# A fused encoder layer: smaller descriptor memory, own bytes for two attention tiles, token scales through DRAM, first tokens in pairs

## The chip, the cores and the metric

The kernel runs on one core of one Trainium2 chip. A core has five engines that run their own instruction streams: TensorE (PE, matrix products; its weight loads are listed as PEld), VectorE (DVE), ScalarE (ACT), GpSimd (POOL) and SyncE (SP), which here issues nearly all DMA transfers. The metric is the device time of one execution in microseconds (us); of several runs the median counts.

## The reference

The kernel computes one layer of a bidirectional encoder for 1280 tokens of width 1024: a prompt of 1024 tokens and a second sequence of 256 that shares the weights. Cut to what matters here:

```python
n = rms_norm(h, g_mix)
qa, ka, va, qb, kb, vb = split(n @ w_in)
# mixer A: 4 heads, two softmax maps each, combined with lambda
sc = einsum(qa, ka) * scale - slope * abs(qpos - kpos)
oa = rms_norm((softmax(sc[0]) - lam * softmax(sc[1])) @ va, g_subln)
# mixer B: 8 query heads on 2 key/value heads
qb, kb = rope(rms_norm(qb, g_qnorm)), rope(rms_norm(kb, g_knorm))
ob = softmax(einsum(qb, kb) * scale) @ vb
h = h + concat(oa, ob) @ w_out
h = h + relu(rms_norm(h, g_mlp) @ w_ff1) ** 2 @ w_ff2
h = h + gate(rms_norm(h, g_ple)) * (p @ w_ple_proj)
return rms_norm(h)
```

All in float32. The norm before the projection is a scale by `g_mix` for each column and by a scalar for each token, the token scale `rstd1`.

## The kernel before, in words

**Arithmetic.** Each float32 operand is split into a high and a low part (`xh`/`xl`, `whp`/`wlp`, `nhi`/`nlo`): ACT writes the high part, DVE (or POOL) the difference. A product is three matmuls, high by high, high by low and low by high (`split3`, L156; `mm_gen`, L225).

**Order.** The program is written with generators that are interleaved; a scheduler with its own timeline then fixes each engine's order, so a change in one place can move rows elsewhere. An engine runs its row in order: an instruction that waits holds everything behind it. SP's transfers use eight semaphores in turn, so each also waits for the one eight before it.

**Start.** `load_w` (L175, L176) loads weights (`rawp`) in pieces of two 128-row blocks and splits them; `load_x` (L239, L240) loads the transposed tokens (`xr`) and makes `xh` (with the scale `gmix`) and `xl`. The first 256 tokens are loaded as two pieces of two blocks and one of four. The unit for the keys and values of mixer B (`b_unit(2, ...)`, output `psb`) takes the first two token blocks together, in two pieces of 12 matmuls each and block. Beside it runs the unit for mixer A's values (`psv`).

**Token scales.** `R` is the row of 1280 token scales on all 128 partitions. It is made with ten diagonal matrices `dg` (DVE, L429), ten products with a matrix of ones (PE, `psr`, L430; 20 records, two for each) and three copies (ACT, L431). Its reader is the eviction `zl<-psa,R` of mixer A's projections (L369, L747).

**Attention.** Keys, queries and values go through DRAM (`kd`, `qd`, `vad`, `vbd`) and come back as tiles `kt`, `qt`, `vt`. Scores `sc` (L559) go to a softmax chain on DVE (`mm`, `rl`), ACT (`p`, `ph`) and POOL, then transposes `tr` (L613) and products with the values (`av`, L637). Keys of mixer B are `kd_72`, its first queries `qd_64` and `qd_65`; mixer A's first are `kd_68` and `qd_60`. `dist` is the table of distances.

**MLP.** The first MLP product is done on quarters of the operands with seven products (i = 1 to 7) for each of 16 pieces p of 256 columns. `mlp_sums` forms sums of transposed tokens (`nb`, `nt`), `n_split` splits them; POOL's DMAs copy parts into `nlo` (L1006). Weight pieces `w1r` (L979) are loaded in turn into the slots W8, W9, W10, multiplied with `gmlp` by POOL (L1046), combined (`w1s`) and split into `w` (L1054, L1055). Products `f_...` are gathered in the tiles `q`, in slots Q0 to Q3 (ACT L1170, DVE L1172 to L1186). Q0 to Q3 and W10 are in one pool `fq` that opens when the pool of `nt` and `nb` closes.

Of the kernel before, what the change touches and what calls it, by code (L numbers as in the profile page):

```python
# [45 lines left out]
def encoder_kernel(ctx: ExitStack, tc: tile.TileContext, x, xT, pT, w_in, w_out, w_ff1, w_ff2, w_gate, w_proj,  # L46
# [44 lines left out]
    def load(*args):  # L91

        with tc.issue_after(chain[-1].ins) if chain else contextlib.nullcontext():
            chain[:] = [dma(*args)]
        return chain[0]
# [32 lines left out]
        return t  # L128

    gmix = cp.tile([P, KD], F32, name="gmix")  # L130
    gmlp = cp.tile([P, KD], F32, name="gmlp")

    neglam = cp.tile([P, 1], F32, name="neglam")
# [19 lines left out]
    def split3(ps, pairs, start=True, stop=True):  # L153
        n = len(pairs)
        for i, (a, b) in enumerate(pairs):
            PE.matmul(ps, a, b, start=start and i == 0, stop=stop and i == n - 1)  # L156
# [5 lines left out]
    def load_w(src, cols, n, rawp, wp, tag, lo_eng, between={}, dma=dma):  # L162

        c0 = cols
        hi, lo = [], []
        kn = 512 // n
        kw = {"bufs": WHB} if n == 256 else {}
        for kk in range(KD // kn):
            if kk in between:
                between[kk]()  # L170
            raw = rawp.tile([P, kn, n], F32, tag="raw", name=f"raw{tag}", bufs=RAWB if n == 256 else 2)
            w_dma[:] = [dma(raw, src[kk * kn * P:(kk + 1) * kn * P, c0:c0 + n].rearrange("(k p) c -> p k c", p=P))]
            a = wp.tile([P, kn, n], F32R, tag="wh", name=f"wh{tag}", **kw)
            b = wp.tile([P, kn, n], F32R, tag="wl", name=f"wl{tag}", **kw)
            S.activation(a, raw, AF.Copy)  # L175
            lo_eng.tensor_tensor(b, raw, f(a[:]), op=ALU.subtract)  # L176
            hi += [a[:, i, :] for i in range(kn)]
            lo += [b[:, i, :] for i in range(kn)]
        return hi, lo


    xs = ExitStack()
# [13 lines left out]
    def pj(name):  # L196
        return ppj.tile([P, 512], F32, tag="pj", name=name)
# [34 lines left out]
    def load_x(t0, n, ks=KD, k1=0, kn=4, dma=dma, tag="xr"):  # L232
        for k0 in range(k1, k1 + ks, kn):
            xr = bp.tile([P, kn, n], F32, tag=tag, name="xr", bufs=2)
            dma(xr, xT[k0 * P:(k0 + kn) * P, t0:t0 + n].rearrange("(k p) t -> p k t", p=P))
            if t0 == k0 == 0:
                load(gmix, g_mix)
            for k in range(k0, k0 + kn):
                S.activation(xh[:, k, t0:t0 + n], xr[:, k - k0], AF.Copy, scale=gmix[:, k:k + 1])  # L239
                V.scalar_tensor_tensor(xl[:, k, t0:t0 + n], xr[:, k - k0], gmix[:, k:k + 1], f(xh[:, k, t0:t0 + n]),  # L240
                                       op0=ALU.mult, op1=ALU.subtract)
# [9 lines left out]
    def tok_pairs(w, t):  # L251
        wh, wl = w
        c = slice(t * P, (t + 1) * P)
        pr = []
        for k in range(KD):
            pr += [(xh[:, k, c], wh[k]), (xh[:, k, c], wl[k]), (xl[:, k, c], wh[k])]
        return pr
# [33 lines left out]
    def b_unit(u, w, hook=None):  # L291

        kv = u == 2
        npair = 1 if kv else 2
        pend = collections.deque()
        pss = {}

        def finish(c0, cn, trp):
            for m in range(npair):
                hl = (bp.tile([P, 2, 512], F32R, tag="qkl", name="qkl", bufs=1) if kv  # L300
                      else bp.tile([P, 2, 512], F32R, tag="xr", name="qkl", bufs=2))
                S.activation(hl[:, 0, :cn], trp[m][:, :cn], AF.Copy)
                V.tensor_tensor(hl[:, 1, :cn], trp[m][:, :cn], f(hl[:, 0, :cn]), op=ALU.subtract)
                dst = kd[4] if kv else qd[4 + 2 * u + m]
                dma(dst[:, :, c0:c0 + cn].rearrange("v p t -> p v t"), f(hl[:, :, :cn]))

        def tr(args):
            o, t, c0, cn, trp = args
            for m in range(npair):
                PE.transpose(trp[m][:, t * P - c0:t * P - c0 + P], o[:, m * P:(m + 1) * P], ident)  # L310
            if (t + 1) * P == c0 + cn:
                finish(c0, cn, trp)

        for (c0, cn) in TCH:
            trp = None
            for t in range(c0 // P, (c0 + cn) // P):
                if hook:
                    hook(t)
                tag = "tr1" if kv and t in (2, 3) else "pb"
                ps = pss.pop(t, None) or pp1.tile([P, 512], F32, tag=tag, name="psb", bufs=2)  # L320
                if kv and t == 0:

                    pss[1] = pp1.tile([P, 512], F32, tag="pb", name="psb", bufs=2)
                    for kh, u_ in itertools.product(range(2), range(2)):
                        split3((ps, pss[1])[u_][:, :256], tok_pairs(w, u_)[12 * kh:12 * kh + 12], kh == 0, kh == 1)
                        yield 1.0
                elif not kv or t != 1:
                    yield from mm_gen(ps[:, :256], tok_pairs(w, t))
                o = norm_rope(ps, t, 2 if kv else 4, gk if kv else gq)
                if kv:  # L330
                    hl = bp.tile([P, 2, 2, 64], F32R, tag="vbl", name="vbl")
                    vps = ps[:, 128:256].rearrange("p (h d) -> p h d", d=64)
                    r1 = rstd1[:, t:t + 1]
                    S.activation(hl[:, :, 0, :], vps, AF.Copy, scale=r1)
                    V.scalar_tensor_tensor(hl[:, :, 1, :], vps, r1, f(hl[:, :, 0, :]),
                                           op0=ALU.mult, op1=ALU.subtract)
                    for j in range(2):
                        dma(vbd[j][t * P:(t + 1) * P, :], f(hl[:, j].rearrange("p v d -> p (v d)")))
                if trp is None:
                    trp = [pp1.tile([P, 512], F32, tag=f"tr{m}", name="trb", bufs=2) for m in range(npair)]  # L340
                if len(pend) == 2:
                    tr(pend.popleft())
                pend.append((o, t, c0, cn, trp))
        while pend:
            tr(pend.popleft())
# [34 lines left out]
    def wload(c, between={}, dma=dma):  # L380
        return load_w(w_in, c, 256, bp, bp, "p", V, between, dma)

    first_x = functools.partial(load_x, 0, 256, dma=load)
    w_kv = wload(2048, {1: lambda: first_x(4, 0, 2), 2: lambda: first_x(4, 4, tag="xt")}, load)
    w_va0 = wload(1024, dma=load)
    stats_x(0, 256, load)
    load_x(256, 256, dma=load)
# [12 lines left out]
    gens = [b_unit(2, w_kv, hook), va_unit(0, w_va0)]  # L400
    for n in range(NT // 2):
        for g in gens:
            for _ in itertools.islice(g, 4 if n == 0 and g is gens[0] else 8):
                pass
    for g in gens:
        drain(g)
# [13 lines left out]
    V.tensor_scalar(neglam, neglam, -LAM_INIT, None, op0=ALU.add)  # L420


    ones = bp.tile([P, P], F32, name="ones", bufs=1)
    V.memset(ones, 1.0)
    for (c0, cn) in TCH:
        ps = pj("psr")
        for t in range(c0 // P, (c0 + cn) // P):
            dg = bp.tile([P, P], F32, tag="dg", name="dg")
            V.tensor_scalar(dg, ident, rstd1[:, t:t + 1], None, op0=ALU.mult)  # L429
            PE.matmul(ps[:, t * P - c0:t * P - c0 + P], ones, dg, start=True, stop=True)  # L430
        S.activation(R[:, c0:c0 + cn], ps[:, :cn], AF.Copy)  # L431

    weave(b_unit(0, wload(1536, dma=load)), va_unit(1, wload(1280, dma=load)), 1.0)
    weave(b_unit(1, wload(1792, dma=load)), qk_a(0), 1.0)
# [30 lines left out]
            fn()  # L465

    def load_k(i, c):
        kt = tl("kt")
        for v in range(2):
            dma(f(kt[v * 64:(v + 1) * 64, :]), kd[i][v, c * 64:(c + 1) * 64, :])  # L470
        return kt
# [5 lines left out]
        return vt  # L477

    def load_q(i, t0):
        qt = tl("qt")  # L480
        for dup in range(2):
            if QM:
                dma(f(qt[dup * 64:(dup + 1) * 64]), qd[i][:, :, t0:t0 + 256].rearrange("v (c d) t -> d c v t", d=64))
                continue
            for c in range(2):
                dma(f(qt[dup * 64:(dup + 1) * 64, c]),
                    qd[i][:, c * 64:(c + 1) * 64, t0:t0 + 256].rearrange("v d t -> d v t"))
        return qt
# [267 lines left out]
            qk_done.append(n)  # L756

    op_state = {}


    slot_pool = {}

    def slot(tag, shape, dt, name):
        return slot_pool[tag].tile(shape, dt, tag=tag, name=name, bufs=1)

    def open_slots(pool_, tags):
        for tag in tags:
            slot_pool[tag] = pool_
            size = {"H": 2560, "L": 2560, "W": 1024, "Q": 1280, "T": 512}[tag[0]]
            slot(tag, [P, size], F32, tag)  # L770

    def open_out_proj():
        xs.close()
# [441 lines left out]
    nts.close()  # L1215
    fqs = ExitStack()
    fq = pool("fq", side="left", stack=fqs)
    open_slots(fq, ["Q0", "Q1", "Q2", "Q3", "W10"])
    w1_load(1, 0)
    w1_load(1, 1)  # L1220
    w1_load(2, 0)
# [333 lines left out]
```

## Time and profile before

| | |
|---|---|
| median of three runs | 1741.91 us (1739.72 to 1742.12) |
| profiled execution | 1741.58 us |
| its span | 1739.8 us |
| mean granted clock of PE | 0.992 |
| PE busy | 1680.0 us (97%), 9868 records |
| DVE, ACT, POOL busy | 1184.3, 860.6, 703.8 us |
| DMA | 262.94 MB, mean 151 GB/s |

The span is the part of the execution between its first and last recorded instruction; the time is 1.8 us more. Busy shares are means over the whole span. A group is written as line, engine, operation, output<-inputs. In the list of waits a row reads: engine, waiting group <- what ended the wait: total us, times, longest us. In a timeline row the first number is the start, the second the duration of the group, and the bracket the idle time before it and what ended it. In the table of stretches a row gives the length, the busy time of each engine with its instructions, the granted clock of PE, the share of the DMA engines and GB/s.

### The profile page before, as it was taken

What the parts mean: (1) busy time and instruction counts of PE and PEld (TensorE: products, weight loads), DVE (VectorE), ACT (ScalarE), POOL (GpSimd) and SP (SyncE); (2) the same over time, 40 slices, a digit from 0 to 9 for tenths busy, and PEclk for the clock granted to TensorE, in tenths of its full rate; (3) what the DMA queues carried; (4) which work ended last, traced back from release to release, by engine and by line L of the source; (5) the groups of instructions that cost most, each with busy time, mean ns of one, the idle gap of its engine ahead of it and who ended that gap; (6) DMA issues with size and microseconds to landing.
All of it is one profiled execution on the core that took longest, in us unless ns stands there. A gap on an engine that the chain in (4) does not pass through costs nothing.

```text
span 1739.8 us, 27306 instructions
## 1 busy us (share of the span) xinstructions
PE 1680.0 (97%) x9868; PEld 1495.8 (86%) x9868; DVE 1184.3 (68%) x2115; ACT 860.6 (49%) x1733; POOL 703.8 (40%) x677
## 2 busy tenths in 40 slices
PE   8999989999989999998999999999999999999997
PEld 8999877888878888877999999998888888888886
DVE  7757477878878778669766666665664865354666
ACT  7522267767777657766333333333333333344554
POOL 1223445645654436355756665630533400001442
PEclk9999999999999999999999999999999999999999
DMA  8723663432773533472443334349676365532111
GB/s 296 239 77 113 178 166 108 120 121 90 227 209 115 156 94 98 127 248 70 167 147 136 133 128 146 135 147 385 220 229 194 119 208 190 181 112 82 40 44 49
DMA packets 187656, 262.94 MB, mean 151 GB/s; under 512 B 13184, under 2 KB 120576, under 8 KB 187520
## 3 DMA queue, kind: packets, MB, share of 16 engines
q1 hardware_dynamic: 185920, 255.95, 45.8%
q0 software_dynamic: 1600, 5.24, 1.0%
q8 instruction: 78, 1.28, 0.3%
q14 instruction: 58, 0.48, 0.1%
HBM read 174.63 MB, written 81.26 MB: 147 GB/s over the span
## 4 chain that ended last, share of the span: by engine, by line
PE 79%; DVE 7%; DMA 6%; ACT 3%; issue 3%; POOL 1%; SPq 1%; POOLq 0%; DVEq 0%; ACTq 0%
PE sc L559 5%; PE psg L156 5%; PE av L637 5%; PE psa L225 5%; PE pso L225 4%; PE tr L613 4%; PE psb L225 3%; PE psv L225 2%; PE psp L156 1%; DMA xt<-in_x 1%; DVE p L594 1%; DVE p L572 1%; DVE pl L624 1%; DVE nlo L1090 1%; DMA h_sb<-in_w_out 1%
## 5 line engine op out<-in xcount | busy, mean ns | idle before, releaser
L559 PE MATMUL sc<-kt,qt 128*128 128x512 f32 (+1 forms) x576 | 157.8, 394 | 16.1 <-ACT p L584 6.6
L1264 ACT ACTIVATE ao<-ar 128x1280 fp32r<-128x1280 f32 x56 | 71.3, 1275 | 189.4 <-PE f__16300 L156 37.8
L1266 DVE TENSOR_TENSOR ao<-ar,ao 128x1280 fp32r<-128x1280 f32 x56 | 95.3, 1704 | 100.2 <-ACT ao L1264 100.1
L624 DVE TENSOR_TENSOR pl<-tr,ph 128x512 fp32r<-128x512 f32 x204 | 138.4, 684 | 33.2 <-ACT ph L619 32.4
L619 ACT ACTIVATE ph<-tr 128x512 fp32r<-128x512 f32 x204 | 120.4, 595 | 66.7 <-PE tr L613 52.9
L559 PEld LDWEIGHTS sc<-kt,qt 128*128 128x128 f32 x576 | 99.4, 190 | 36.9 <-ACT p L584 9.2
L225 PE MATMUL pso<-ow,mt 128*128 128x512 f32 x480 | 123.9, 402 | 3.8 <-DMA mt<-md 2.2
L613 PE MATMUL tr<-ident,p 128*128 128x128 f32 x768 | 117.0, 276 | 8.1 <-DVE pl L624 7.4
L1046 POOL TENSOR_SCALAR w1r<-w1r,gmlp 128x256 f32<-128x256 f32 x128 | 104.7, 834 | 42.0 <-DMA w1r<-in_w_ff 39.6
L156 PE MATMUL psg<-gw,n 128*128 128x512 f32 (+1 forms) x504 | 115.2, 384 | 0.0
L613 PEld LDWEIGHTS tr<-ident,p 128*128 128x128 f32 x768 | 92.6, 142 | 25.5 <-DVE pl L624 9.1
L156 PEld LDWEIGHTS psg<-gw,n 128*128 128x128 f32 x504 | 90.8, 188 | 19.5
L225 PEld LDWEIGHTS pso<-ow,mt 128*128 128x128 f32 x480 | 87.8, 190 | 21.4 <-DMA mt<-md 2.5
L637 PE MATMUL av<-ph,vt 128*128 128x256 f32 x544 | 102.4, 290 | 1.7 <-ACT ph L619 0.7
L1054 ACT ACTIVATE w<-w1s 128x512 fp32r<-128x512 f32 x64 | 40.1, 628 | 121.7 <-POOL w1s L1061 6.5
L598 POOL TENSOR_SCALAR p<-p,rl 128x1024 f32<-128x1024 f32 x64 | 75.3, 1179 | 52.5 <-DVE rl L596 52.2
L576 DVE TENSOR_REDUCE mm<-sc 128x1 f32<-128x1024 f32 (+1 forms) x80 | 83.9, 1055 | 10.4 <-PE sc L559 10.0
L637 PE MATMUL av<-pl,vt 128*128 128x256 f32 x408 | 90.0, 302 | 0.1
L637 PEld LDWEIGHTS av<-ph,vt 128*128 128x128 f32 x544 | 82.4, 190 | 7.3 <-ACT ph L619 1.1
L572 DVE CUSTOM_DVE_ANT_0 p<-sc,dist 128x1024 f32<-128x1024 f32 x64 | 77.4, 1217 | 9.8 <-PE sc L559 4.6
L1439 POOL TENSOR_TENSOR p_l<-pr,p_h 128x256 fp32r<-128x256 f32 x10 | 7.8, 781 | 184.0 <-ACT p_h L1438 184.0
L584 ACT ACTIVATE p<-sc,mm 128x1024 f32<-128x1024 f32 x64 | 71.3, 1114 | 19.9 <-DVE mm L576 11.0
(1511 smaller groups left out, 4805.3 us busy)
## 6 DMA issues: line engine op xcount, KB each, us to landing
ar<-ad SPq DMA_DIRECT2D x56, 640.0 KB, 4.1
w2r<-in_w_ff SPq DMA_DIRECT2D x56, 512.0 KB, 4.4
qt<-qd SPq DMA_DIRECT2D x160, 128.0 KB, 3.0
ad<-q SPq DMA_DIRECT2D x64, 320.0 KB, 2.2
w1r<-in_w_ff SPq DMA_DIRECT2D x32, 512.0 KB, 3.9
ad<-qs SPq DMA_DIRECT2D x48, 320.0 KB, 2.2
md<-ml SPq DMA_DIRECT2D x40, 256.0 KB, 2.6
mt<-md SPq DMA_DIRECT2D x20, 512.0 KB, 4.9
```

The source lines that it names most:

```text
L156: PE.matmul(ps, a, b, start=start and i == 0, stop=stop and i == n - 1)
L225: PE.matmul(ps, a, b, start=i == 0, stop=i == n - 1)
L559: PE.matmul(ps[:, h0:h0 + n], shared["q"][:, cc, v, i * P:(i + 1) * P], kt[:, s0 + h0:s0 + h0 + n], start=v == 0, stop=v == 1)
L572: V.tensor_tensor_reduce(out=p[:, :sn], in0=ps[:, :sn], in1=dst_t[:, off:off + sn], scale=SLOPES[idx], scalar=3.0e38, op0=ALU.add, op1=ALU ...
L576: V.tensor_reduce(out=st["m", i][:, 0:1], in_=ps[:, :sn], axis=AX.X, op=ALU.max, negate=True)
L598: G.tensor_scalar(p[:, :sn], p[:, :sn], rl[:, 0:1], 1.0, op0=ALU.mult, op1=ALU.mult)
L613: PE.transpose(t[:, jj, i * P:(i + 1) * P], st["ws"][i][:, j * P:(j + 1) * P], ident)
L619: S.activation(ph, st["tr", j2], AF.Copy)
L624: V.tensor_tensor(pl, st["tr", j2], f(st["ph", j2][:]), op=ALU.subtract)
L637: PE.matmul(st["av"][:, :256], x_, y_, start=j2 == 0 and n == 0, stop=j2 == nj - 1 and n == len(pr) - 1)
L1046: G.tensor_scalar(r, r, gmlp[:, k:k + 1], 1.0, op0=ALU.mult, op1=ALU.mult)
L1266: V.tensor_tensor(ao[:, 1], a, f(ao[:, 0]), op=ALU.subtract)
```

## The change

Five parts:

1. `gmix` is loaded from ACT's queue at the program's start, and no longer in SP's row between the first two pieces of x.
2. The second half of the first tokens is loaded in two pieces, after the second and the third piece of weights. The first two token blocks are done in four pieces of six matmuls each instead of two of twelve, and the unit's first turn is eight steps instead of four.
3. The diagonal matrices, the products `psr` and the copies of `R` are gone. `rstd1` is written to a DRAM tile `rd` (1280 elements of 4 bytes) and read back into `R` on all partitions.
4. The descriptor memory of POOL's DMAs is 4096 instead of 16384 bytes of each partition.
5. Of the 12288 bytes that this leaves, 10240 hold the slots Q0 and Q1 from the start. They take the first keys `kt` and the first queries `qt` of mixer B (i = 4), and later the MLP's `q`. The pool `fq` opens with Q2, Q3 and W10 alone, so W10 has another address: it now lies over bytes of `nb` and `nt`, where it lay over those of `hn` before.

```diff
     gmix = cp.tile([P, KD], F32, name="gmix")
+    S.dma_start(gmix, g_mix)
...
+    open_slots(pool("fz", side="left"), ["Q0", "Q1"])
...
             dma(xr, xT[k0 * P:(k0 + kn) * P, t0:t0 + n].rearrange("(k p) t -> p k t", p=P))
-            if t0 == k0 == 0:
-                load(gmix, g_mix)
...
-                    for kh, u_ in itertools.product(range(2), range(2)):
-                        split3((ps, pss[1])[u_][:, :256], tok_pairs(w, u_)[12 * kh:12 * kh + 12], kh == 0, kh == 1)
+                    for kq, u_ in itertools.product(range(4), range(2)):
+                        split3((ps, pss[1])[u_][:, :256], tok_pairs(w, u_)[6 * kq:6 * kq + 6], kq == 0, kq == 3)
                         yield 1.0
...
-    w_kv = wload(2048, {1: lambda: first_x(4, 0, 2), 2: lambda: first_x(4, 4, tag="xt")}, load)
+    w_kv = wload(2048, {1: lambda: first_x(4, 0, 2), 2: lambda: first_x(2, 4, 2, tag="xt"),
+                        3: lambda: first_x(2, 6, 2, tag="xt")}, load)
...
-            for _ in itertools.islice(g, 4 if n == 0 and g is gens[0] else 8):
+            for _ in itertools.islice(g, 8):
...
-    ones = bp.tile([P, P], F32, name="ones", bufs=1)
-    V.memset(ones, 1.0)
-    for (c0, cn) in TCH:
-        ps = pj("psr")
-        for t in range(c0 // P, (c0 + cn) // P):
-            dg = bp.tile([P, P], F32, tag="dg", name="dg")
-            V.tensor_scalar(dg, ident, rstd1[:, t:t + 1], None, op0=ALU.mult)
-            PE.matmul(ps[:, t * P - c0:t * P - c0 + P], ones, dg, start=True, stop=True)
-        S.activation(R[:, c0:c0 + cn], ps[:, :cn], AF.Copy)
+    rd = dp.tile([1, T], F32, name="rd")
+    dma(rd.rearrange("a (t p) -> p (a t)", p=P), rstd1)
+    dma(R, rd.to_broadcast([P, T]))
...
-        kt = tl("kt")
+        kt = slot("Q0", [P, T], F32R, "kt") if i == 4 and c == 0 else tl("kt")
...
-        qt = tl("qt")
+        qt = slot("Q1", [P, 2, 2, 256], F32R, "qt") if i == 4 and t0 == 0 else tl("qt")
...
-    open_slots(fq, ["Q0", "Q1", "Q2", "Q3", "W10"])
+    open_slots(fq, ["Q2", "Q3", "W10"])
...
-    nc = _bacc.Bacc("TRN2", target_bir_lowering=False, num_devices=1)
+    nc = _bacc.Bacc("TRN2", target_bir_lowering=False, num_devices=1, dynamic_dma_scratch_size=4096)
```

**SP where R is loaded.** The piece of SP's row near 65 us, first before, then with the change. `rawp` and `rawa` are weights, `vad` and `vbd` stores of values, `rd` and `R` the token scales.

```order
L357 DMA vad_74<-vl 128x256
L94 DMA rawp<-in_w_in 128x2x256
L338 DMA vbd_77<-vbl 128x128
L338 DMA vbd_78<-vbl 128x128
L94 DMA rawp<-in_w_in 128x2x256 x3
L94 DMA rawa<-in_w_in 128x4x128
```
```order
L439 DMA rd<-rstd_95 128x10x1
L94 DMA rawp<-in_w_in 128x2x256
L371 DMA vad_73<-vl 128x256
L371 DMA vad_74<-vl 128x256
L94 DMA rawp<-in_w_in 128x2x256 x2
L440 DMA R<-rd 128x1280
L94 DMA rawp<-in_w_in 128x2x256
L352 DMA vbd_77<-vbl 128x128
L352 DMA vbd_78<-vbl 128x128
L94 DMA rawp<-in_w_in 128x2x256 x3
L94 DMA rawa<-in_w_in 128x4x128
```

`R<-rd` waits for the store `rd` to land; four loads of `rawp`, two stores and the first `rawa` stand behind it.

**SP where the first keys and queries are loaded.** Before, the piece near 200 us; then, with the change, the piece where mixer B's `kt` stands now (behind the last store of `kd_72`), the one with its `qt`, and what is left near 200 us.

```order
L750 DMA kd_69<-zl 128x2x512
L305 DMA qd_66<-qkl 128x2x256
L305 DMA qd_67<-qkl 128x2x256
L921 DMA dist<-in_dist 128x1920
L470 DMA kt<-kd_72 64x1280 x2
L750 DMA kd_69<-zl 128x2x512
L486 DMA qt<-qd_64 64x2x256
L714 DMA rawq<-in_w_in 128x4x128
L486 DMA qt<-qd_64 64x2x256 x2
L750 DMA kd_69<-zl 128x2x256
```
```order
L319 DMA kd_72<-qkl 128x2x256
L371 DMA vad_76<-vl 128x256
L724 DMA rawq<-in_w_in 128x4x128
L480 DMA kt<-kd_72 64x1280 x2
L371 DMA vad_75<-vl 128x256
...
L319 DMA qd_64<-qkl 128x2x512
L319 DMA qd_65<-qkl 128x2x512
L496 DMA qt<-qd_64 64x2x256 x3
```
```order
L919 DMA dist<-in_dist 128x1920
L486 DMA vt_3063<-vbd_77 128x10x128
L480 DMA kt<-kd_68 64x1280
L760 DMA kd_69<-zl 128x2x512
L480 DMA kt<-kd_68 64x1280
L724 DMA rawq<-in_w_in 128x4x128
L480 DMA kt<-kd_68 64x1280 x2
L496 DMA qt<-qd_60 64x2x256
L760 DMA kd_69<-zl 128x2x256
L496 DMA qt<-qd_60 64x2x256 x3
```

Mixer B's first two `kt` and four `qt` (the fourth a few rows on) stand 41 and 28 rows ahead of `dist`; behind `dist` mixer A's `kt` and `qt` follow at once, between the stores of `kd_69`.

**POOL where the MLP begins.** Before, then with the change: the multiplications of `w1r` and the sums `w1s` of the second piece.

```order
L1006 DMA nlo_9721<-nb 128x4x128
L1046 TENSOR_SCALAR w1r<-w1r,gmlp 128x256 x12
L1060 TENSOR_TENSOR w1s<-w1r 128x512
L1061 TENSOR_TENSOR w1s<-w1r,w1s 128x512
L1070 TENSOR_TENSOR w1s<-w1r,w1s 128x512
L1055 TENSOR_TENSOR w_10515<-w1r,w_10515 128x512
```
```order
L1004 DMA nlo_9693<-nb 128x4x128
L1044 TENSOR_SCALAR w1r<-w1r,gmlp 128x256 x8
L1053 TENSOR_TENSOR w_10485<-w1r,w_10485 128x512
L1053 TENSOR_TENSOR w_10529<-w1r,w_10529 128x512
L1044 TENSOR_SCALAR w1r<-w1r,gmlp 128x256 x4
L1058 TENSOR_TENSOR w1s<-w1r 128x512
L1059 TENSOR_TENSOR w1s<-w1r,w1s 128x512
```

Twelve multiplications in a run become eight, two `w`, and the four of the piece in W10, whose load waits until the last `nlo<-nt` on DVE is done; the sums `w1s` stand behind them.

More of the change, by code (lines that the diff above doesn't have):

```diff
@@ L179, in load_w, with slot, open_slots @@
         return hi, lo
+    slot_pool = {}
+    def slot(tag, shape, dt, name):
+        return slot_pool[tag].tile(shape, dt, tag=tag, name=name, bufs=1)
+    def open_slots(pool_, tags):
+        for tag in tags:
+            slot_pool[tag] = pool_
+            size = {"H": 2560, "L": 2560, "W": 1024, "Q": 1280, "T": 512}[tag[0]]
+            slot(tag, [P, size], F32, tag)
+    open_slots(pool("fz", side="left"), ["Q0", "Q1"])
     xs = ExitStack()
@@ L758, in encoder_kernel @@
     op_state = {}
[L761 to L770, printed above, removed]
     def open_out_proj():
```

## The prediction

> **What bounds the kernel now.** I read the busy shares first, then the waits of TensorE (PE), then the stretches that the change touches. The page's busy shares, and the waits of PE (engine, waiting group, releaser; us in total, times, longest):
>
> ```profile
> PE 1680.0 (97%) x9868; PEld 1495.8 (86%) x9868; DVE 1184.3 (68%) x2115; ACT 860.6 (49%) x1733; POOL 703.8 (40%) x677
> ...
> PE tr L613 <- DVE pl L624: 7.6, 11, 1.4
> PE sc L559 <- ACT p L584: 6.6, 7, 1.7
> PE psb L156 <- ACT xh L239: 5.3, 1, 5.3
> PE sc L559 <- DVE mm L572: 4.2, 9, 1.2
> PE sc L559 <- DMA qt<-qd: 4.1, 1, 4.1
> PE f__10465 L156 <- ACT q L1170: 3.4, 1, 3.4
> PE psr L430 <- DVE dg L429: 2.3, 2, 1.8
> ```
>
> PE is the bound: 97% busy, and nothing else comes near. A change can only remove PE work or one of these single waits. Five places are touched: the start, the R stretch near 70 us, the first scores near 220, the MLP's start near 810, and the descriptor ring behind POOL's DMAs.
>
> **(a) The start.** The timeline (start, us, engine, line, group, [idle before, releaser]), and PE with its granted clock and the DMA share in four stretches:
>
> ```profile
> 0.74 1.28 ACT L116 ACT_TABLE_LOAD   x1 [0.74 <-PEq L1546]
> ...
> 1.75 0.46 SPq L94 DMA_DIRECT2D gmix<-in_g_mix  x1
> ...
> 4.76 0.91 ACT L239 ACTIVATE xh<-xr,gmix 128x256 fp32r<-128x256 f32 x2 [0.57 <-DMA gmix<-in_g_mix]
> ...
> 10.04 1.70 ACT L239 ACTIVATE xh<-xr,gmix 128x256 fp32r<-128x256 f32 x4 [2.58 <-DMA xr<-in_xT]
> ...
> 12.32 0.75 PE L156 MATMUL psb<-whp,xh 128*128 128x256 f32 x2 [2.28 <-ACT whp L175]
> ```
> ```profile
> 5.30:8.90 3.60, 3.57 (x16) 1.00 0.92 273
> 12.30:15.70 3.40, 3.38 (x14) 0.51 0.92 352
> 15.70:19.00 3.30, 3.30 (x30) 0.98 0.90 313
> ...
> 20.00:40.00 20.00, 20.00 (x173) 20.00 (x172) 17.87 (x84) 17.59 (x54) 3.65 (x8) 1.00 0.97 339
> ```
>
> Moving gmix to ACT's queue gains nothing for gmix itself: ACT issues it after its table load, at 2.02 instead of 1.75, so the first matmul moves by about +0.3. But SP's later loads go out 0.5 us sooner. Splitting the second half of x matters more. Today PE stands 2.28 us until four xh (1.70 us) and a whp have run behind one 512 KB transfer. In halves, two xh suffice (0.91 instead of 1.70, so 0.8 less), and half the bytes (0.26 MB at 273 GB/s, 1.0 us) need to have landed. Sum: +0.3 − 0.5 − 0.8 − 1.0 = **−2.0**. Bounds: −0.5 if the third piece waits as long as the whole did; −4 if the gap closes and with it the slow stretch behind it (14 matmuls at 0.24 us instead of 0.11, 1.8 us). I stay at −2.0, since at 20 to 40 us the DMA share is 0.97: the next tokens' transfers can't follow much faster, and a PE further ahead would meet them.
>
> [...]
>
> **(b) R.** PE near 70 us, the first reader of R, and ACT's wait for weights behind the same SP queue:
>
> ```profile
> 69.77 0.61 PE L430 MATMUL psr<-dg,ones 128*128 128x128 f32 x4
> 70.13 0.37 PE L225 MATMUL psb<-wlp,xh 128*128 128x256 f32 x1
> ```
> ```profile
> 73.21 0.63 ACT L175 ACTIVATE wha<-rawa 128x512 fp32r<-128x512 f32 x1 [2.48 <-DMA rawa<-in_w_in]
> ```
> ```profile
> L369 DVE SCALAR_TENSOR_TENSOR zl<-psa,R x6: 411/680/682, 145.2 to 191.8; 128x512 f32<-128x512 f32 x4, 128x256 f32<-128x256 f32 x2
> ```
> ```profile
> gmix<-in_g_mix SPq DMA_DIRECT2D x1, 4.0 KB, 2.9
> ```
>
> Four psr records take 0.36 us of PE's queue, 0.09 each; the twenty that go are 1.8 us. The psr waits, 2.3 us, go too: −4.1. Ten dg and three R copies leave engines with room. R is first read at 145 us, so its own landing is covered by some 70 us. What it costs is SP's order: R<-rd stands until rd has landed. The nearest row for 4-byte elements is gmix, 1024 of them in 2.9 us; rd has 1280 and two loads are issued in between, so SP stands 1 to 3 us. R's 0.66 MB then share the engines with the weights. Queued behind are rawp and rawa; ACT's wha waits for rawa today, with PE's evictions in line behind it. I charge 0.6: **−3.5**. Bounds: −4.1, and 0 if evictions are late by all that was gained.
>
> [...]
>
> **(c) Keys and queries.** A quiet and a full stretch of the DMA engines, SP's issues, and PE at the first scores:
>
> ```profile
> 100.00:120.00 20.00, 20.00 (x174) 20.00 (x174) 12.49 (x36) 5.07 (x15) 4.41 (x6) 1.00 0.30 107
> ...
> 200.00:220.00 20.00, 18.54 (x94) 15.44 (x92) 5.61 (x8) 5.22 (x10) 7.04 (x7) 1.00 1.01 270
> ```
> ```profile
> 202.50 1.17 SPq L470 DMA_DIRECT2D kt<-kd  x2
> ...
> 210.07 0.54 SPq L750 DMA_DIRECT2D kd<-zl  x1
> ...
> 215.25 5.01 SPq L486 DMA_DIRECT2D qt<-qd  x4
> ```
> ```profile
> 220.16 2.32 PE L559 MATMUL sc<-kt,qt 128*128 128x512 f32 x8 [1.62 <-ACT p L584]
> ...
> 226.84 1.55 PE L559 MATMUL sc<-kt,qt 128*128 128x512 f32 x4 [4.14 <-DMA qt<-qd]
> ```
>
> From 200 us the DMA engines are full, and mixer A's qt, issued last, land when PE has stood 4.14 us. In the new order mixer B's first kt (two of 320 KB) and qt (four of 128 KB) leave this stretch: kt goes out behind the last kd, qt behind the first qd, where the share is 0.3. 1.18 MB less at 270 GB/s is 4.4 us, so A's qt land near 222.4. B's first scores come earlier, among projection matmuls, so the 1.62 (scores waiting on the softmax ahead of them) is covered too and PE is there at 222.7 − 1.6 = 221.1. It then waits 1.3 instead of 5.76: −4.5. SP still holds for the kd<-zl store at 210.07, which POOL sets; this leaves A's qt about where I put them. **−4.5**; −5.8 if they land in time, −2.5 if A's loads, held by these stores, come forward by only 2.5.
>
> **(d) The MLP's start.** POOL, DVE and PE near 810 us, and the landing of the three w1r loads issued at 798 to 799 us (min/median/max):
>
> ```profile
> 802.08 14.40 POOL L1046 TENSOR_SCALAR w1r<-w1r,gmlp 128x256 f32<-128x256 f32 x12 [15.98 <-DMA w1r<-in_w_ff]
> ```
> ```profile
> 809.89 1.48 DVE L1090 TENSOR_TENSOR nlo<-nt,nhi 128x512 fp32r<-128x512 f32 x2
> ```
> ```profile
> 811.06 2.06 PE L156 MATMUL f__10465<-nhi,w 128*128 128x256 f32 x8 [3.36 <-ACT q L1170]
> ...
> 824.78 1.58 PE L156 MATMUL f__10637<-nhi,w 128*128 128x384 f32 x8
> ```
> ```profile
> DMA to landing us min/median/max: 3.9/4.9/5.8
> ```
>
> With Q0 and Q1 there from the start, PSUM is evicted earlier and the 3.36 goes. But W10 now lies over bytes of nb and nt, and its load must wait for the last nlo<-nt, which in the new order has some 4 us of q additions ahead of it: 811.4 + 4 = 815.4. It lands at the least 3.9 later, 819.3; POOL's four multiplications (14.40/12 = 1.2 each) end at 824.1, the first w1s and its copy near 826. PE, 3.36 us ahead, wants that weight at 824.78 − 3.36 = 821.4 and so stands some 4 us. −3.4 + 3.9 = **+0.5**; bounds −3.4 (the DVE reaches it without delay) and +3.
>
> **(e) The ring.** A quarter of the descriptor memory, behind POOL's twenty nlo transfers of 256 KB:
>
> ```profile
> q0 software_dynamic: 1600, 5.24, 1.0%
> ```
> ```profile
> L1006 POOL DMA_DIRECT2D nlo<-nb x9: 747/747/948, 745.9 to 785.3; - x9
> ```
> ```profile
> nlo<-nb POOLq DMA_DIRECT2D x9, 256.0 KB, 5.9
> ```
>
> 1600 packets over 20 transfers and 16 engines are five each, and eight in flight are forty. At **0** I assume that they fit; up to +3 otherwise. Attention's reordered instructions between 200 and 480 us: 0, with 2 us either way.
>
> Sum: −2.0 − 3.5 − 4.5 + 0.5 = −9.5; from the profiled execution's 1741.58, **1732.1** (1732.4 against the median 1741.91, 0.3 above).
>
> **Rivals.**
> 1. *The clock stays low at the start* (chance 0.10). Short pauses between the pieces: 34 further matmuls, up to the end of the first values, at 0.24 instead of 0.11 cost 4.4: 1736.5. For it: 0.51 after one pause. Against: the pieces' pauses should be under 2.28.
> 2. *The gains were hidden anyway* (0.17). DMA-bound start −0.5, R given back by late evictions 0, A's keys bound by SP's stores −2.5, W10 late +2.6: 1741.2. For it: shares of 0.97 and 1.01, where a wait removed is met again at the next transfer.
> 3. *Softmax without cover* (0.07). B's first units run among projections, so projection matmuls that covered later softmax steps are spent; the three softmax waits (7.6 + 6.6 + 4.2 = 18.4) grow. The kernel is slower from 13 us of growth (9.5 that it gives back and 3.5 more, some 70%); doubled they give 1732.1 + 18.4 = 1750.5. Against: the work ahead of A's first scores is the same in both orders.
> 4. *The ring stops POOL* (0.04). With n transfers in flight twenty take 20 × 5.9/n = 118/n us; the stretch has 39.4. At four nothing is lost; at two 59 − 39.4 = 19.6 are: 1751.7. Against: a quarter of a memory that held forty packets need not hold fewer than twenty.
>
> **How the numbers follow.** Forecast 0.62; with rival 1, which is still faster by more than 0.2% (3.5 us, about what one can tell from no change), 0.72; same 0.17; slower 0.11. The forecast's own range: 1727 to 1737. Down, (a) and (c) at their better bounds with (d) kept give 1728.8, the order another 2: 1726.5. Up, I include rival 2, to 1741.5, and leave out 3 and 4.
>
> **What would show it.** (a) right: the gap before the third piece under 0.6 us, no stretch at half clock behind it; wrong: two pauses over 1 us. (b): psr gone, SP standing 1 to 3 us before R's load, no PE wait over 1 us between 60 and 80. (c): A's first scores waiting under 2 us; wrong if the wait for qt stays near 4. (d): a wait of 3 to 5 us on a w at the MLP's second group in place of the 3.36. (e): POOL's issues still 0.75 us. A softmax wait sum above 25 us would make rival 3 the cause, and idle time before nlo near 800 us rival 4.

## The result, and the profile after

| | before | with the change |
|---|---|---|
| median, timed together | 1742.01 us (1739.72 to 1743.78) | 1732.76 us (1731.98 to 1734.35) |
| ratio, with its 95% interval | | 0.9949 [0.9932, 0.9966] |
| profiled execution, its span | 1741.58, 1739.8 us | 1731.98, 1730.2 us |
| PE busy | 1680.0 us | 1676.3 us |

The change makes the kernel faster by 9.3 us between the medians, where 9.5 were forecast. The sum was right, and that is luck: of its terms one had the wrong sign, one was less than half of what it should have been, one gain does not reach the end at all, and one cost is 3 us larger. They happen to cancel, and most of what follows is about that.

The waits of PE over the whole run, with the change (engine, waiting group, releaser; us in total, times, longest):

```profile
PE trb L324 <- DVE ro L302: 9.2, 2, 7.9
PE sc L569 <- ACT p L594: 5.2, 6, 1.7
PE psb L157 <- ACT xh L253: 5.0, 1, 5.0
PE sc L569 <- DVE mm L582: 3.6, 8, 1.2
PE tr L623 <- DVE pl L634: 3.5, 7, 1.1
```

The waits for `whp` at the start (2.3), `qt` (4.1), `psr` (2.3) and `f__10465` (3.4) have left the list. At its head stands a new one, larger than any part of the forecast allowed for: one stand of 7.9 us at `trb`, the transposes of mixer B's keys.

The change gains time before the MLP and loses some in it. These are the transposes `tr` of the attention, in the kernel before and with the change (min/median/max ns, start of the first and of the last):

```profile
L613 PE MATMUL tr<-ident,p x768: 270/272/421, 222.3 to 737.9; 128*128 128x128 f32 x192
L623 PE MATMUL tr<-ident,p x768: 270/272/331, 218.9 to 724.8; 128*128 128x128 f32 x192
```

The last one starts 13.1 us sooner, and behind it PE has the same work in both kernels; yet from there to the end of the span it is 1001.9 us before and 1005.4 with the change. So 13.1 us are gained up to the end of the attention, and 3.5 are lost behind it.

**The start.** Timeline rows, and PE with the change in one stretch (length, PE busy, granted clock, DMA share, GB/s):

```profile
0.74 1.28 ACT L116 ACT_TABLE_LOAD   x1 [0.74 <-PEq L1544]
...
0.77 0.43 ACTq L131 DMA_DIRECT2D gmix<-in_g_mix  x1
...
4.96 0.58 PE L157 MATMUL psb<-whp,xh 128*128 128x256 f32 x1 [4.96 <-ACT xh L253]
```
```profile
12.00:15.70 3.70, 3.70 (x34) 1.00 1.02 378
```

The gap before the third piece is closed, not shortened, and the slow stretch behind it is gone: 34 matmuls in 3.7 us where the kernel before had 14 in 3.4. `gmix` was issued at 0.77, beside ACT's table load and not after it.

How much of this the change earned is less clear than the two traces make it look. `ring_only` (below) has the instructions of the kernel before in the same order. PE from 5.3 to 19 us before, in `ring_only`, and with the change:

```profile
5.30:19.00 13.70, 11.39 (x66) 0.88 0.95 325
5.30:19.00 13.70, 12.65 (x87) 1.00 0.96 340
5.30:19.00 13.70, 13.70 (x99) 1.00 0.96 345
```

`ring_only` has neither the gap nor the slow stretch. Over all traces of this case the old start does 63 to 88 matmuls here (six traces, median 81.5) and the new one 84 to 106 (eight traces, median 99.5). At 0.11 us for each, the start is worth some 2 us; against the profiled execution of before alone it looks like 4.

**R.** PE at the end of its stand, ACT's row just before, and the transfers issued between 59 and 72 us (KB each, median us to landing):

```profile
74.29 0.47 PE L324 MATMUL trb<-ident,ro 128*128 128x128 f32 x1 [7.94 <-DVE ro L302]
```
```profile
71.53 0.63 ACT L176 ACTIVATE whp<-rawp 128x512 fp32r<-128x512 f32 x1 [9.08 <-DMA rawp<-in_w_in]
```
```profile
rawp<-in_w_in SPq DMA_DIRECT2D x4, 256.0 KB, 11.6
R<-rd SPq DMA_DIRECT2D x1, 640.0 KB, 5.3
vad<-vl SPq DMA_DIRECT2D x2, 128.0 KB, 13.1
rd<-rstd SPq DMA_DIRECT2D x1, 5.0 KB, 12.2
```

The 5 KB store `rd` takes 12.2 us to land, and the weights and values issued around it take as long. ACT, which works in order, stands 9 us at a weight's split; the eviction and the norm that PE's transposes need are behind it. In stretches (PE, PEld, DVE, ACT and POOL busy, PE's granted clock, DMA share, GB/s), with the change:

```profile
55.00:59.00 4.00, 2.78 (x24) 2.58 (x23) 2.54 (x14) 2.00 (x6) 0.00 (x0) 1.00 1.03 340
63.00:67.00 4.00, 3.35 (x29) 3.15 (x27) 0.51 (x3) 0.00 (x0) 0.46 (x1) 1.00 0.87 68
67.00:71.50 4.50, 0.00 (x0) 0.00 (x0) 0.00 (x0) 0.00 (x0) 0.00 (x0) 0.98 1.04 100
```

From 63 to 71.5 the DMA engines are busy 87% and more and move 68 to 100 GB/s; from 55 to 59 they moved 340 at 103%. SP stood 5.2 us for `rd` before it issued `R<-rd` at 71.37, where the forecast had 1 to 3.

**The MLP's start.** POOL, PE, and the landing of the `w1r` loads issued between 780 and 810 us:

```profile
807.56 2.52 POOL L1044 TENSOR_SCALAR w1r<-w1r,gmlp 128x256 f32<-128x256 f32 x4 [0.96 <-DVE q L1178]
```
```profile
810.80 0.44 PE L157 MATMUL f__10564<-nhi,w 128*128 128x384 f32 x1 [1.24 <-ACT w L1052]
...
812.60 0.69 PE L157 MATMUL f__10638<-nhi,w 128*128 128x384 f32 x1 [1.24 <-ACT w L1052]
...
814.30 1.97 PE L157 MATMUL f__10564<-nhi,w 128*128 128x384 f32 x5 [0.80 <-DVE w L1053]
```
```profile
w1r<-in_w_ff SPq DMA_DIRECT2D x3, 512.0 KB, 4.0
```

1.24 + 1.24 + 0.80 = 3.3 us of waits on `w` in place of the 3.36 on `q`. But these waits are not all that changed here. PE from the end of the last `tr` on, for as many matmuls, before and with the change (length, PE busy, granted clock, DMA share, GB/s):

```profile
738.20:841.10 102.90, 93.32 (x531) 0.95 0.50 161
725.10:832.10 107.00, 95.85 (x532) 0.94 0.49 158
```

With the change they take 4.1 us more: 1.6 of it is idle time, and for 2.5 PE is busy longer with the same work. From there to the end of the span the kernel with the change takes 0.6 us less, which leaves the 3.5.

### The profile page after: what moved, and what is told of

Same layout as the page of the kernel before. It is cut to its first block, busy times and chain, and to the rows that moved or that the text cites. A ratio compares the mean times of both kernels' runs of the same rounds, so it can differ in the third digit from the quotient of the medians.

```text
span 1730.2 us, 27230 instructions
## 1 busy us (share of the span) xinstructions
PE 1676.3 (97%) x9848; PEld 1493.9 (86%) x9848; DVE 1180.3 (68%) x2104; ACT 859.7 (50%) x1730; POOL 703.0 (41%) x677
## 4 chain that ended last, share of the span: by engine, by line
PE 85%; DVE 5%; issue 3%; DMA 3%; ACT 2%; POOL 1%; SPq 0%; POOLq 0%; DVEq 0%; ACTq 0%
PE psa L241 6%; PE sc L569 6%; PE av L647 5%; PE psg L157 5%; PE pso L241 5%; PE psb L241 4%; PE tr L623 4%; PE psv L241 3%; PE psp L157 1%; DMA rawp<-in_w_in 1%; DMA h_sb<-in_w_out 1%; DVE pl L634 1%; DVE p L604 1%; PE f__16266 L157 1%; PE f__15226 L157 1%
## 5 line engine op out<-in xcount | busy, mean ns | idle before, releaser
L1044 POOL TENSOR_SCALAR w1r<-w1r,gmlp 128x256 f32<-128x256 f32 x128 | 108.4, 863 | 38.5 <-DMA w1r<-in_w_ff 19.0
```

The lines of the kernel that those rows point to most:

```text
L1044: G.tensor_scalar(r, r, gmlp[:, k:k + 1], 1.0, op0=ALU.mult, op1=ALU.mult)
```

## The experiments

Each kernel was timed beside the kernel before on the same chip; ratios are to that. The kernel with the change stands at 0.9949.

### What makes PE stand near 70 us

`psr_back` takes part 3 back:

```diff
-    rd = dp.tile([1, T], F32, name="rd")
-    dma(rd.rearrange("a (t p) -> p (a t)", p=P), rstd1)
-    dma(R, rd.to_broadcast([P, T]))
+    ones = ...    # dg, psr and the copies of R as in the kernel before
```

> Part 3 undone: the diagonal matrices, psr and the copies of R are back; all else as in the changed kernel. Theory A (the 4-byte store rd clogs the DMA engines, and PE's 7.9 us wait near 70 us is the price): that wait and the 1.2 us ahead of it shrink to what the kernel before had (0.5 on trb), psr's 1.8 us of PE and some 2.3 us of waits on dg return: 1732.8 - 8.7 + 4.1 = about 1728. Rival B (the wait comes from the earlier start, which runs PE ahead of its weights): the wait stays near 8 us and psr's cost comes on top: about 1737.

1731.51 us (1728.52 to 1733.22), ratio 0.9937 [0.9923, 0.9952]. The stand of 7.9 us is gone; the longest wait near 70 us is 1.6. So the early start is not its cause (rival B). The gain, 1.3 us between the medians with overlapping intervals, is smaller than expected; `rd_rows`, next, is 8 us faster than this kernel. Their profiled executions differ by 7.4 us, and the traces say where: the last `tr` starts at 719.3 us in `psr_back` and at 714.3 in `rd_rows`, 5.0 us for the way through psr; the other 2.4 lie behind it, in the MLP, which neither edit touches.

`rd_rows` keeps the way through DRAM and changes the form of the store:

```diff
+    rps = pj("rps")
+    PE.transpose(rps[:NT, :P], rstd1, ident)
+    rrow = bp.tile([NT, P], F32, name="rrow", bufs=1)
+    V.tensor_copy(rrow, rps[:NT, :P])
-    dma(rd.rearrange("a (t p) -> p (a t)", p=P), rstd1)
+    dma(rd.rearrange("a (t p) -> (a t) p", p=P), rrow)
     dma(R, rd.to_broadcast([P, T]))
```

> As the changed kernel, but rstd1 (128x10) is first transposed on PE to 10x128 and stored as ten rows of 512 bytes instead of 1280 elements of 4 bytes; R is read back as before. Theory A: the store lands in 2 to 4 us instead of 12.2, weights issued beside it land in 5 to 6 us instead of 12 to 13, PE's 7.9 us wait falls under 1 us: 1732.8 - 7.5 = about 1725. Rival B (PE is ahead of its weights in any case): the wait stays above 5 us, 1731 or more. Rival C (SP's stand at R<-rd is what delays the weights, not the form of the store): weights issued before the stand still land late, the wait falls by half at most: 1728 to 1730.

1723.47 us (1721.08 to 1724.11), ratio 0.9891 [0.9876, 0.9905]: 9.3 us faster than the kernel with the change. SP's issues, and all waits of PE in the first 110 us:

```profile
69.79 0.36 SPq L443 DMA_DIRECT2D rd<-rrow  x1
...
72.25 0.50 SPq L444 DMA_DIRECT2D R<-rd  x1
```
```profile
PE psb L157 <- ACT xh L253: 5.0, 1, 5.0
PE trb L324 <- DVE ro L302: 0.4, 1, 0.4
```

R's load, which waits for the store, goes out 2.46 us after it: the same 5 KB in ten rows of 512 bytes have landed by then. That is more than the wait of 7.9 us gives, because the clock goes with it. PE from 74 to 78 us, with the change and in `rd_rows` (length, PE busy, granted clock, DMA share, GB/s):

```profile
74.00:78.00 4.00, 3.71 (x18) 0.50 0.98 345
```
```profile
74.00:78.00 4.00, 3.86 (x33) 1.00 0.89 297
```

After a stand of 7.9 us PE restarts at half clock and does 18 matmuls where 33 fit: 1.8 us more.

`rd_late` keeps the 4-byte store and moves it to a quiet time:

```diff
+    rz = bp.tile([P, NT], F32, name="rz", bufs=1)
+    dma(rz, kd[4][0, :, T - NT:])
+    V.scalar_tensor_tensor(rz, rz, 0.0, rstd1, op0=ALU.mult, op1=ALU.add)
-    dma(rd.rearrange("a (t p) -> p (a t)", p=P), rstd1)
+    dma(rd.rearrange("a (t p) -> p (a t)", p=P), rz)
```

> As the changed kernel, with the 4-byte store, but the stored scales are made with a small load of the last keys of mixer B (times zero, added), so that rd can't be stored before some 85 us, where the DMA share is low. Theory A: the store again takes about 10 us and slows what is issued beside it, but near 85 to 100 us nothing on PE's path waits for it: the 7.9 us wait is gone, 1725 to 1727. Rival D (the clog depends on the full DMA engines near 60 us, not on the store): rd lands in 3 to 4 us there. Rival B: the wait stays near 70 us, 1732.

1725.08 us (1723.84 to 1725.27), ratio 0.9901 [0.9886, 0.9916]. The transfers issued between 83 and 94 us:

```profile
vad<-vl SPq DMA_DIRECT2D x2, 128.0 KB, 6.6
rd<-rz SPq DMA_DIRECT2D x1, 5.0 KB, 10.2
```

The store takes 10.2 us with little else under way (58 GB/s in mean over these 11 us, 0.64 MB in all), so the full DMA engines near 60 us are not its cause (rival D). The same 5 KB in ten rows took under 2.5, so in these runs it is slow by its form; and at this time, with no weights issued beside it, it costs the path some 8 us less than with the change. The two stores of 128 KB beside it take 6.6 us; those that `rd_rows` issues between 83 and 94 us take 1.7. SP's stand alone (rival C) is not the cause either: in the kernel with the change the weights that were issued after the store and before R's load already took 11.4 to 12.9 us. A stand of 2.2 us of PE on a value's eviction near 97 us remains in `rd_late`.

`rd_only` is the kernel before with part 3 alone.

> The kernel before with part 3 alone (the 4-byte store and the load of R for the diagonal matrices and psr). Theory A: 4.1 us of psr leave, the wait near 70 us comes, shorter by the 4 us by which PE arrives later than in the changed kernel, with a slow restart: -4.1 + 4 to 6 + 1.8 = 1743 to 1746, not faster. Rival (the prediction's price): 1738.

1743.43 us (1742.08 to 1745.80), ratio 1.0009 [0.9999, 1.0019]. Its trace has the stand:

```profile
PE trb L310 <- DVE ro L288: 5.9, 1, 5.9
```

Alone, part 3 gains nothing (+1.6 us by the ratio, −0.2 to +3.3 by its interval), where the forecast gave it −3.5.

### What the start is worth

`start_back` undoes parts 1 and 2 in the kernel with the change; `rows_start_back` does so in `rd_rows`.

```diff
-    S.dma_start(gmix, g_mix)
+            if t0 == k0 == 0:
+                load(gmix, g_mix)
...
-                    for kq, u_ in itertools.product(range(4), range(2)):
+                    for kh, u_ in itertools.product(range(2), range(2)):
...
-2: lambda: first_x(2, 4, 2, tag="xt"), 3: lambda: first_x(2, 6, 2, tag="xt")
+2: lambda: first_x(4, 4, tag="xt")
```

> Parts 1 and 2 undone: gmix on SP's queue, the second half of the first x in one piece, two pieces of twelve matmuls; all else as in the changed kernel. Theory of the trace: first matmul at 5.3 instead of 5.0, the wait of 2.3 us and the slow stretch behind it (1.8) return, 4.4 us in all, but PE then meets the slow weights near 70 us 4.4 us later and waits for them that much less: 1733 to 1734, hardly slower than the changed kernel. Rival (the gain at the start is kept to the end): 1732.8 + 4.4 = 1737.

1732.73 us (1731.30 to 1734.26), ratio 0.9945 [0.9927, 0.9962]: the same as with the change. PE at the end of the stand near 70 us:

```profile
74.54 0.47 PE L325 MATMUL trb<-ident,ro 128*128 128x128 f32 x1 [6.49 <-DVE ro L303]
```

The stand ends at 74.5 instead of 74.3, whenever PE arrived: the weights set that time, and the whole gain of the start was spent waiting for them. (The 2.3 us gap and the slow stretch that were expected back did not come: this trace has a gap of 1.0 us and no stretch at half clock.)

> rd_rows with parts 1 and 2 undone. With the slow weights gone there should be nothing near 70 us to give the start's gain back to. Theory (the gain at the start was taken by the wait near 70 us, which ends at the same time whenever PE arrives): the start now counts: 1723.2 + 3 to 4.4 = 1726 to 1728. Rival (a second floor behind it, transfers of x or weights between 20 and 60 us): 1723 to 1724 again.

1727.48 us (1725.14 to 1727.88), ratio 0.9913 [0.9890, 0.9936], against 1723.47 with the new start. With the stand gone the start counts, some 4 us; the two intervals overlap a little, so the size is less certain than the medians make it look. In the traces 2.7 us of the difference are there at the last `tr` (717.0 against 714.3), and 1.4 come behind it, where parts 1 and 2 change nothing.

### What the keys' and queries' own bytes are worth

`kq_back` loads mixer B's first kt and qt into their old tiles; `kq_only` is the kernel before with parts 4 and 5 alone.

```diff
-        kt = slot("Q0", [P, T], F32R, "kt") if i == 4 and c == 0 else tl("kt")
+        kt = tl("kt")
...
-        qt = slot("Q1", [P, 2, 2, 256], F32R, "qt") if i == 4 and t0 == 0 else tl("qt")
+        qt = tl("qt")
```

> Mixer B's first kt and qt are back in their old tiles; Q0 and Q1 stay open from the start for the MLP alone. Theory of the prediction: the waits of 4.1 (qt) and 1.6 us at the first scores return: 1732.8 + 5.8 = 1738.5. Rival E (the 5 us that the softmax waits between 240 and 760 us lost come from these tiles too, by the order that they allow): these waits return as well, 1743. Rival F (the early start alone had made the qt wait vanish): no change, 1733.

1747.21 us (1745.16 to 1750.34), ratio 1.0032 [1.0020, 1.0045]: slower than the kernel before, and 14.5 us slower than with the change, more than rival E allowed.

> The kernel before with parts 4 and 5 alone (descriptor memory, Q0 and Q1 from the start with the first keys and queries in them); the start and psr as before. Theory E (5.8 us of waits at the first scores, some 5 of softmax waits between 240 and 310, and nothing at the MLP's start): 1742 - 10.8 = 1731. Prediction's term: 1742 - 4.5 + 0.5 = 1738. Rival (the gain depends on the earlier start): 1740.

1733.88 us (1732.17 to 1735.01), ratio 0.9957 [0.9941, 0.9972]. All waits of PE from 210 to 320 us, in the kernel before, in `kq_back`, and with the change:

```profile
PE sc L559 <- DMA qt<-qd: 4.1, 1, 4.1
PE tr L613 <- DVE pl L624: 3.3, 3, 1.4
PE psa L225 <- DVE o L685: 2.3, 2, 1.4
PE sc L559 <- ACT p L584: 1.6, 1, 1.6
PE sc L559 <- DVE mm L572: 0.7, 2, 0.4
```
```profile
PE tr L623 <- DVE pl L634: 3.3, 3, 1.4
PE psa L241 <- DVE o L695: 2.3, 2, 1.4
PE sc L569 <- DMA qt<-qd: 1.9, 1, 1.9
PE sc L569 <- ACT p L594: 1.6, 1, 1.6
PE sc L569 <- DVE mm L582: 0.7, 2, 0.4
```
```profile
PE psa L241 <- DVE o L695: 0.6, 1, 0.6
```

12.0 us before, 9.8 with the tiles taken back, 0.6 with the change (0.6 in `kq_only` too). Both undoing and doing the part alone move the same waits, so they belong to it: not only the wait for qt, but 6 us of waits on the softmax behind it, to the tenth the same rows as before. The waits are not the whole of it. The last `tr` starts 12.5 us later in `kq_back` than with the change (737.3 against 724.8), and 15.6 us sooner in `kq_only` than before (722.3 against 737.9); some 1.6 of the 12.5 are there by 130 us (937 matmuls against 951). What lies between these times and the waits is left open.

`kq_only` reaches 7.5 us at the end rather than the 10.8 expected because it loses at the MLP's start: behind its last `tr` the span has 1008.1 us, where the kernel before has 1001.9. Two waits at the MLP's first products, 3.5 on `w` and 2.0 on `nhi`, are the largest there; the wait for `mt` near 760 us is 3.4 (2.2 before).

### The MLP's start, and the ring

`w10_first` and `w10_mid` are `rd_rows` with another order in the pool, so that W10's load waits for earlier sums:

```diff
-    open_slots(fq, ["Q2", "Q3", "W10"])
+    open_slots(fq, ["W10", "Q2", "Q3"])     # w10_first
+    open_slots(fq, ["Q2", "W10", "Q3"])     # w10_mid
```

> As rd_rows, with the pool of the MLP's tiles opened in the order W10, Q2, Q3 instead of Q2, Q3, W10, so that W10 lies over other bytes of nb and its load waits for an earlier sum on DVE (six instructions sooner) instead of the last nlo<-nt. Theory G (the MLP's start waits because W10's bytes come free late): the load is issued some 3 us sooner and the waits on w near 800 us (1.2 + 2.9) shrink by 2 to 4 us: 1723.5 - 3 = 1720.5. Rival H (POOL's row or DVE is the limit there): the same time, 1723.5, or the wait moves to Q2 or Q3.

> As rd_rows, with the order Q2, W10, Q3: the load of W10 waits for a sum on DVE ten instructions sooner, and for a split on ACT. Theory G: as w10_first or a little better, 1719 to 1721. Rival H: 1723.5.

1723.15 us, ratio 0.9888 [0.9872, 0.9904], and 1722.93 us, 0.9890 [0.9872, 0.9908]: no gain over 1723.47. In `w10_mid` the multiplications follow without a wait, and PE still stands. POOL, DVE, and PE's wait:

```profile
794.66 2.00 POOL L1048 TENSOR_SCALAR w1r<-w1r,gmlp 128x256 f32<-128x256 f32 x4
```
```profile
797.17 1.55 DVE L1200 TENSOR_TENSOR qs<-q 128x640 f32<-128x640 f32 x1 [1.10 <-ACT q L1164]
798.75 1.78 DVE L1202 TENSOR_TENSOR qs<-q,qs 128x640 f32<-128x640 f32 x1
800.45 1.88 DVE L1204 TENSOR_TENSOR q<-q 128x640 f32<-128x640 f32 x1
802.25 0.68 DVE L1057 TENSOR_TENSOR w<-w1r,w 128x512 fp32r<-128x512 f32 x1
```
```profile
PE f__10568 L157 <- DVE w L1057: 3.7, 1, 3.7
```

The weight's low part stands behind three sums of 640 columns in DVE's row. `w1_pool` takes it out of that row:

```diff
-        split(1, a11)
+        split(1, a11, G if p == 1 else V)
```

> As w10_mid, and the low part of the first weight of the MLP's second piece is made by POOL instead of DVE, where it stands behind three sums of 640 columns (5 us). Theory I (DVE's row, not the late load, sets the wait of 3.7 us there): POOL makes it some 3 us sooner, the wait on that w falls to about 1 us: 1722.9 - 2.7 = about 1720. Rival (POOL's later sums w1s, 1.4 us later each, take its place): 1722 to 1723.

1719.11 us (1718.24 to 1720.92), ratio 0.9860 [0.9844, 0.9877], the best version here, faster than both kernels. The wait on that weight:

```profile
PE f__10568 L157 <- POOL w L1057: 0.6, 1, 0.6
```

3.7 us became 0.6: DVE's row was the limit once the load came early. (The intervals of the two ratios touch.) Whether this edit alone, with the late load, would do as much was not tried.

The time from the last `tr` to the end of the span shows the price of the MLP's start over all traces. It is 1001.6 to 1002.6 us in the three kernels without part 5 (before, `ring_only`, `rd_only`) and 1004.4 to 1008.1 in the ten that have it, or in `kq_back` its slots alone, and split that weight on DVE. In `w1_pool` it is 1001.7: the loss is gone.

`ring_only` is the kernel before with `dynamic_dma_scratch_size=4096` alone.

> The kernel before with the descriptor memory of 4096 bytes and nothing else; the order of all instructions is the same. Prediction: no difference, 1742 within 1. Rival (POOL's transfers wait for descriptors): POOL's issues longer than 0.75 us, nlo transfers later, up to +3.

1742.10 us (1739.03 to 1743.75), ratio 0.9996 [0.9987, 1.0005]: nothing.

## Why the prediction was right in its sum and wrong in its terms

The span shrank by 9.6 us. PE's rows tell where, term by term:

| term | forecast | what the traces show |
|---|---|---|
| (a) start | −2.0 | some −2 over all traces (−4 against the one of before), all lost by 75 us |
| (b) R | −3.5 | −4.1 (psr), then +8.7 of waits on `trb` and +1.8 of slow clock: +6.4 |
| (c) keys, queries | −4.5 | −11.4 in waits from 210 to 320 us (12.0 to 0.6); −14.4 up to the last `tr` |
| (d) MLP | +0.5 | −0.1 in the waits that it names (3.36 to 3.3); +3.5 in all |
| (e) ring | 0 | 0 |

The start's gain is counted in (a) and its loss in (b), since PE's stand is longer by what PE came earlier. Both together are +1.3: by 130 us PE has done 951 matmuls with the change and, without the 20 of psr, 962 before, and 174 of them take 20 us from 100 to 120 us. That is about 1 us less than −4 and +6.4 add up to, which stays open. Then −14.4 up to the last `tr`, and +3.5 behind it: −9.6.

**(a)** had the right size and rested on shaky ground: the gap of 2.28 us and the slow stretch from which it was read are those of one execution, and `ring_only` shows neither. Wrong was the step "a PE further ahead would meet" the next tokens' transfers: no wait shows up between 5 and 56 us. But what PE then met was (b)'s late weights. Also wrong was "ACT issues it after its table load, at 2.02": it went out at 0.77. The clock rival did not come true with the new start: PE's granted clock was 1.00 from 5.3 to 19 us. `rd_only`, with the old one, shows something like it: with pauses of 0.3 and 0.8 us its matmuls come only every 0.21 us from the start up to 16 us.

**(b)** is the step that failed. It rested on "the nearest row for 4-byte elements is gmix, 1024 of them in 2.9 us". That row was misread: gmix arrives as 128 rows of 32 bytes. With the change it has a queue of its own, and in the first four microseconds that queue shows 144 packets in all, 128 of them of 32 bytes:

```profile
q10 hardware_dynamic: 144, 0.00, 2.0%
```

So the trace of before held no row for such a store, and the bound on the bad side was set at "given back" instead of "worse than before". (There are also not "two loads" between `rd` and `R<-rd`: SP's row has three loads and two stores there.) What the runs show is the time of two forms of the same 5 KB: 12.2 (with the change) and 10.2 us (`rd_late`) in 4-byte elements, under 2.5 (`rd_rows`) in rows of 512 bytes. Where between the two sizes the change lies, and by what mechanism, they do not show. The second half of the step, that SP's stand is what costs, was wrong too: it is the transfers beside the store that are slowed, those issued before the stand included (11.4 to 12.9 us for 256 KB, 4.8 to 5.7 for those issued from R's load on).

**(c)** had the mechanism and mis-sized it. 4.1 and 1.6 us at the first scores went as worked out, by loads that left the full stretch. Another 5.7 us are waits on the softmax between 240 and 310 us, which the sum put at "0, with 2 us either way" as the effect of a reordered row. They go and come with the two tiles, and so does some of the time between these 11.4 us and the 14.4, which no row here explains. Why, is argued and not shown: with its keys there early, mixer B's first softmax runs among projections, and later steps are no longer in phase with mixer A's.

**(d)** named the right waits and left out the rest. The load of W10 was indeed issued late, and PE stood 3.3 us on `w`; but PE was also busy 2.5 us longer with the same matmuls, and +3.5 lies beyond the bound of +3. `w10_mid` shows that DVE's row holds the same wait without the late load, and `w1_pool` that most of the 3.5 us hang on this row: 1004.4 us behind the last `tr` in `w10_mid`, 1001.7 with the split on POOL. The working has a slip besides: 826 − 821.4 is 4.6 and not 3.9, which would have made the term +1.2. (At the lower end of the range, 1728.8 less 2 is 1726.8 and not 1726.5.)

**Rival 2** (hidden gains) described (a)'s fate well, though it had another place for it, and its +2.6 for (d) was nearer than the forecast's +0.5. **Rival 3** (softmax without cover) was wrong in sign: its three waits went from 18.4 to 12.3 us. **Rival 4** is excluded by `ring_only` (ratio 0.9996). The forty packets of (e) are an estimate, for eight transfers in flight: the trace of before has at most six of POOL's at once, and what a packet takes of the descriptor memory no run shows.

## What to carry to other kernels

A store's form can cost more than its bytes: here 5 KB took 12.2 and 10.2 us as 1280 elements of 4 bytes and under 2.5 as ten rows of 512 bytes, for one transpose on PE and one copy on DVE. Try both forms of a small store, and look at what is in flight beside it. A gain ahead of a point where PE waits for a transfer can be worth nothing until that wait is gone (the start: 1732.73 without it and 1732.76 us with it while PE stood near 70 us, 1727.48 and 1723.47 without the stand); test early-stage edits after the later floor is removed, or undo one at a time and look where the traces meet again. When a nearest row is to price an unseen operation, check its packets, not its element count. And a list of waits is not the whole price of a stretch: compare the time between two events that both traces have.

## What the runs showed of the hardware that was not expected

- 1280 elements of 4 bytes stored to DRAM took 12.2 us to land beside other traffic and 10.2 with little else under way; the same 5 KB in ten rows less than 2.5. Beside the first, transfers of 256 KB took 11.4 to 12.9 us, where those issued from 71.8 to 75.3 us took 4.8 to 5.7, and the DMA engines showed 87 to 104% busy at 68 to 100 GB/s from 63 to 71.5 us.
- A DMA issued from ACT's queue went out at 0.77 us, while ACT's table load ran from 0.74 to 2.02.
- After a stand of 7.9 us PE's granted clock was 0.50 from 74 to 78 us, 1.8 us of work lost. After the 2.3 us gap of the kernel before it was 0.51 for 3.4 us, again 1.8 us of work, so that wait cost 4.1 us, nearly twice its length. Not every gap does: in `start_back` 27 matmuls followed a gap of 1.0 us in the same 3.4 us, against 14 before. In `rd_only` 14 followed a gap of 0.8, so the length of the gap alone does not decide.
- The same instructions in the same order did 66 matmuls between 5.3 and 19 us in one execution (before) and 87 in another (`ring_only`). One profiled execution of a start is not enough to price it.
